# The low halves of the weight tiles: a negated cast and an adding DMA in place of a subtraction

## The chip, the cores and the metric

One core of a Trainium2 chip runs the whole program. Its engines are TensorE (matmul), VectorE, ScalarE and GpSimd; SyncE (SP) only issues transfers here. The metric is the device time of one execution in microseconds.

## The reference

Two layers of a decoder trunk over 512 tokens of width 1024, all in float32. Each layer is a token mixer with three attention branches, three gates and an output projection, and then a channel mixer with a causal convolution of width 3.

```
for i in range(DEPTH):                       # DEPTH = 2
    h = rms_norm(x, attn_norm[i])
    proj = h @ w_in[i]                       # 1024 x 5376
    ...                                      # attention A, B, C: ya, yb, yc
    g = jax.nn.sigmoid(gates.reshape(B, S, N_BRANCH, D))
    merged = g[:, :, 0] * (ya @ w_pa[i]) + g[:, :, 1] * (yb @ w_pb[i]) + g[:, :, 2] * (yc @ w_pc[i])
    x = x + merged @ w_out[i]                # 1024 x 1024
    h = rms_norm(x, mlp_norm[i])
    u = causal_depthwise_conv(h @ w_up[i], conv_w[i], conv_b[i])   # 1024 x 5632
    gate_u, val_u = jnp.split(u, 2, axis=-1)
    x = x + (jax.nn.silu(gate_u) * val_u) @ w_down[i]              # 2816 x 1024
```

Per layer that is 5.4 M weights in w_in, 1 M in the branch projections, 1 M in w_out, 5.8 M in w_up and 2.9 M in w_down, 129 MB in both layers. The rest of the work, the attention, is small at 512 tokens.

## The kernel before, in words

Every float32 operand of a large product is split in two numbers of the type float32r: a high half, the operand rounded to that type, and a low half, operand minus high half. A product is then three matmuls, high by high, high by low and low by high, all added up in PSUM.

Weights come as tiles of 128 x 1024 numbers, 512 KB: for most matrices two groups of 128 rows by 512 columns, for the value columns of w_in four groups by 256, for w_up two groups by two pieces of 256 columns, one from the gate half and one from the value half. There are 246 tiles. `w_dma` has SP load a tile into one of two `raw` buffers, in one transfer, or in two for w_up. `w_prep` makes `whi` by a cast on ScalarE and `wlo` by a subtraction on VectorE or GpSimd; each of the two has four buffers (NW). `dense` walks the blocks of tiles in order and issues, tile by tile, 4 column chunks x 2 row groups x 3 matmuls of 512 columns, so 24 for a tile (48 of 256 columns for the value tiles). At the start of tile i of a block it calls `pump`, which prepares tiles up to i + 2 and has SP load two more.

What runs beside the dense blocks (norms, attention, rotary) are generators. The loop at the end of `trunk` takes the next piece of work from them by an estimate of each engine's clock (class `Estimate`), so the order of instructions on every engine is fixed when the program is built, and a change of an instruction's price in `Estimate.note` moves others. On the chip each engine runs its instructions in that order and waits at each for what it needs.

GpSimd's other work are powers and copies of small statistics: `rn` for the norms (`norm_tail`, line 552), `rr`, `rq`, `nrq`, `rk` for the heads' norms (`rstd_tb`), and the tables of the rotary step. In before all transfers are issued from SP and, for a few constants, ScalarE. The program is opened with room for descriptors of GpSimd's own transfers, in bytes of each partition:

```
nc = _bacc.Bacc("TRN2", target_bir_lowering=False, num_devices=1, dynamic_dma_scratch_size=1024)   # line 1641
```

Nearly every instruction is issued through `Clocked.run`, so the profile puts nearly all of them on line 168 and the names of the tiles tell them apart: `raw`, `whi`, `wlo` are the weights, `d` the PSUM banks of the dense products, `h` the split normed activations, `slot` the general buffers of 128 x 1024, `temp` those of 128 x 512, `tp` and `s` the PSUM of transposes and scores.

Of the kernel before, what the change touches and what calls it, by code (L numbers as in the profile page):

```python
# [11 lines left out]
F32 = mybir.dt.float32  # L12
F32R = mybir.dt.float32r
AF = mybir.ActivationFunctionType
OP = mybir.AluOpType
# [14 lines left out]
POOL_LEAD = 3  # L30
POOL_BIAS = -1000000000.0
# [96 lines left out]
class Bufs:  # L128
# [21 lines left out]
    def any(self, n=1):  # L150
        return len(self.free) >= n
# [3 lines left out]


class Clocked:
    """Runs an engine's instructions and keeps an estimate of when each one ends."""

    def __init__(self, est, eng, key):  # L160
        self._est, self._eng, self._key = est, eng, key
# [12 lines left out]
class Estimate:  # L174
# [60 lines left out]
    def note(self, key, op, args, kw):  # L235
        aps = [x for x in list(args) + list(kw.values()) if isinstance(x, bass.AP)]
        out = kw.get("out", args[0] if args else None)
        if not isinstance(out, bass.AP):
            return
        outs = [out]  # L240
        if "accum_out" in kw and kw["accum_out"] is not None:
            outs.append(kw["accum_out"])
        if op == "tensor_tensor_reduce":
            outs.append(args[-1])
        ins = [x for x in aps if not any(x is o for o in outs)]
        t = self.clock[key]
        for x in ins:
            t = max(t, self.written.get(x.tensor.name, 0.0) + self.SEM)
        for o in outs:
            nm = o.tensor.name  # L250
            if key != "PE" and op != "dma_start":
                t = max(t, self.written.get(nm, 0.0) + (self.SEM if nm in self.written else 0.0))
            if nm[:2] in ("h0", "h1"):
                t = max(t, self.used.get(nm, 0.0) + self.SEM)
            if nm in self.pred:
                t = max(t, self.used.get(self.pred.pop(nm), 0.0) + self.SEM)
        if op == "dma_start":
            self.clock[key] = t + 0.06
            go = max(t + 0.1, self.clock["DGE"])
            self.clock["DGE"] = go + (0.475 if key == "SP" else 0.66)  # L260
            self.clock["DMA"] = max(self.clock["DMA"], go + 1.1) + 1.456 * out.size() / 131072
            end = self.clock["DMA"] + 0.75
        else:
            two = False
            if self.lock and key in ("DVE", "POOL"):
                sb = [x.space != bass.MemoryType.PSUM for x in ins if x.free_size() > 1]
                if key == "POOL":
                    two = any(sb)
                else:
                    two = sum(sb) > 1 or (op in ("tensor_copy", "tensor_scalar") and all(sb)  # L270
                                          and out.space != bass.MemoryType.PSUM)
            if two:
                for s, e in self.port["POOL" if key == "DVE" else "DVE"]:
                    if s <= t < e:
                        t = e
            end = t + self.cost(key, op, out, ins, kw, args)
            self.clock[key] = end
            if two:
                self.port[key].append((t, end))
        self.last = (t, end)  # L280
        for x in ins + outs:
            nm = x.tensor.name
            self.used[nm] = max(self.used.get(nm, 0.0), end)
        for o in outs:
            self.written[o.tensor.name] = max(self.written.get(o.tensor.name, 0.0), end)
# [40 lines left out]
def trunk(ctx: ExitStack, tc: tile.TileContext, out: bass.AP, a: dict):  # L326
    core = tc.nc
    est = Estimate()
# [32 lines left out]
    threads = []  # L361
# [134 lines left out]
    def first_part(t, j):  # L496
        sl = slice(t * 128, (t + 1) * 128)
        ps = tps.get()
        for c in range(4):
            nc.tensor.transpose(ps[:, c, :], X[t][:, (4 * j + c) * 128:(4 * j + c + 1) * 128], identf)  # L500
        for c in range(4):
            k = 4 * j + c
            nc.scalar.activation(H[0, k][:, sl], ps[:, c, :], AF.Copy, scale=gain(0, k))
        for c in range(0, 4, 2):
            nc.scalar.copy(XT[2 * j + c // 2].rearrange("p (e t) -> p e t", e=2)[:, :, sl], ps[:, c:c + 2, :])
        for c in range(4):
            k = 4 * j + c
            nc.vector.scalar_tensor_tensor(H[1, k][:, sl], ps[:, c, :], gain(0, k), H[0, k][:, sl].bitcast(F32),
                                           op0=OP.mult, op1=OP.subtract)
        tps.put(ps)  # L510
# [99 lines left out]
    wt = []  # L610
    W = {}
    RAW = {}
    state = {"dma": 0, "prep": 0, "fin": 0, "busy": False}
# [20 lines left out]
    def w_prep(j):  # L634
        hi = est.alloc("whi", NW, wpool.tile([128, 1024], F32R, tag="whi", name="whi"))
        lo = est.alloc("wlo", NW, wpool.tile([128, 1024], F32R, tag="wlo", name="wlo"))
        raw = RAW.pop(j)
        nc.scalar.copy(hi, raw)
        if state["busy"]:
            t = est.ready(hi)  # L640
            pool = max(est.clock["POOL"], t) <= max(est.clock["DVE"], t) + POOL_BIAS
        else:
            pool = threads[1:] and est.clock["POOL"] <= est.clock["PE"] + POOL_LEAD
        if pool:
            nc.gpsimd.tensor_sub(lo, raw, hi.bitcast(F32))
        else:
            nc.vector.tensor_sub(lo, raw, hi.bitcast(F32))
        if j in wide:
            slots.put(raw)
        if j < 2:  # L650
            first_part(0, j)
        W[j] = (hi, lo)

    def pump(lead):
        while state["prep"] < min(state["fin"] + NW, lead, len(wt)):
            while state["dma"] < min(state["prep"] + ahead(), len(wt)):
                w_dma(state["dma"])
                state["dma"] += 1
            w_prep(state["prep"])
            state["prep"] += 1  # L660
        while state["dma"] < min(state["prep"] + ahead(), len(wt)):
            w_dma(state["dma"])
            state["dma"] += 1
# [888 lines left out]
    def eng_clock(eng):  # L1552
        if eng == "ANY":
            return min(est.clock["ACT"], est.clock["DVE"])
        return est.clock[eng]
# [6 lines left out]
    while threads:  # L1562
# [24 lines left out]
        for r, th in others:  # L1587
            c = eng_clock(th.cur[0])
# [62 lines left out]
```

## Time and profile before

| | us |
|---|---|
| median of the 2 runs | 1603.82 |
| the runs | 1603.31 and 1604.33 |
| span of the profiled execution | 1599.4 |
| busy: TensorE, VectorE, ScalarE, GpSimd | 1546.0, 1077.5, 789.8, 293.6 |

The span goes from the first instruction to the last; the profiled execution's own device time is not listed apart, and the span lies 4.4 us below the median. Busy time of TensorE is that of matmuls that overlap in its pipeline, so 97% busy does not mean 97% of what the engine can do. By stage the program is: layer 0 mixer to about 365 us, gates' end, projections and w_out to about 450, w_up to about 690, w_down to about 810, and the same again for layer 1.

### The profile page before, as it was taken

How to read it: one execution, taken by the hardware profiler on the slowest of the kernel's cores; microseconds unless marked ns; L12 is line 12 of the kernel's file. 1: busy time of each engine (PE TensorE's matmuls, PEld its weight loads, DVE VectorE, ACT ScalarE, POOL GpSimd, SP SyncE). 2: the span in 40 equal slices, each digit the busy share in tenths (PEclk: the TensorE clock that was granted, in tenths of full speed). 3: DMA queues.
4: the chain of work that ended last, by engine and by line, in shares of the span. 5: the costliest groups of instructions: out<-in, count | busy, mean ns of one | idle time of the engine just before them, and what ended most of it. 6: DMA issues, size and time to landing. Idle time of an engine off the chain costs nothing.

```text
span 1599.4 us, 21003 instructions
## 1 busy us (share of the span) xinstructions
PE 1546.0 (97%) x7584; PEld 1283.9 (80%) x7584; DVE 1077.5 (67%) x2242; ACT 789.8 (49%) x1534; POOL 293.6 (18%) x243
## 2 busy tenths in 40 slices
PE   8999999999999999999998999999999999999999
PEld 6777787778878888888887887878788788888887
DVE  5998888988576655543269898797875856665321
ACT  7565656755344444333155666647634544443220
POOL 3443343321010000000044553323200100000000
PEclk9999999999999999999999999999999999999999
DMA  5423152223233233333332224322242233223331
GB/s 176 150 57 90 54 198 67 68 65 132 86 100 100 86 105 106 106 99 125 92 113 66 80 67 158 93 80 64 69 151 87 79 106 93 89 83 106 118 119 53
DMA packets 115495, 157.21 MB, mean 98 GB/s; under 512 B 18880, under 2 KB 71104, under 8 KB 115392
## 3 DMA queue, kind: packets, MB, share of 16 engines
q1 hardware_dynamic: 102768, 153.19, 30.6%
q10 hardware_dynamic: 12624, 2.69, 0.8%
q8 instruction: 60, 0.98, 0.2%
q14 instruction: 43, 0.35, 0.1%
HBM read 144.84 MB, written 11.01 MB: 97 GB/s over the span
## 4 chain that ended last, share of the span: by engine, by line
PE 73%; DVE 20%; ACT 3%; issue 2%; POOL 1%; DMA 0%; ACTq 0%; SPq 0%; DVEq 0%; POOLq 0%
PE d L168 67%; DVE slot L168 8%; PE tp L168 5%; DVE temp L168 4%; DVE s L168 2%; ACT slot L168 2%; DVE nb L168 2%; PE s L168 1%; DVE rl L168 1%; DVE wlo L168 1%; DVE h L168 1%; POOL rr L168 1%; ACT whi L168 1%; ACT temp L168 0%; DMA raw<-in_w_in 0%
## 5 line engine op out<-in xcount | busy, mean ns | idle before, releaser
L168 PE MATMUL d<-h,whi 128*128 128x512 f32 x2176 | 683.0, 395 | 8.6 <-DVE h L168 4.5
L168 PEld LDWEIGHTS d<-h,whi 128*128 128x128 f32 x2176 | 399.9, 189 | 88.5 <-DVE h L168 5.6
L168 PE MATMUL d<-h,wlo 128*128 128x512 f32 x1088 | 425.9, 391 | 0.0
L168 DVE TENSOR_TENSOR wlo<-raw,whi 128x1024 fp32r<-128x1024 f32 x174 | 211.1, 1225 | 263.3 <-ACT whi L168 263.1
L168 ACT CAST whi<-raw 128x1024 fp32r<-128x1024 f32 x246 | 256.1, 1051 | 267.1 <-PE d L168 131.8
L168 PE MATMUL d<-slot,whi 128*128 128x512 f32 x864 | 266.6, 390 | 0.0
L168 POOL TENSOR_TENSOR wlo<-raw,whi 128x1024 fp32r<-128x1024 f32 x72 | 175.5, 2438 | 407.9 <-ACT whi L168 368.0
L168 PEld LDWEIGHTS d<-h,wlo 128*128 128x128 f32 x1088 | 204.9, 188 | 44.0 <-DVE wlo L168 0.2
L168 PE MATMUL d<-whi,h 128*128 128x512 f32 (+1 forms) x768 | 207.4, 344 | 0.4 <-ACT h L168 0.4
L168 PEld LDWEIGHTS d<-slot,whi 128*128 128x128 f32 x864 | 161.6, 188 | 33.3
L168 DVE SCALAR_TENSOR_TENSOR temp<-d,packed,temp 128x511 f32<-128x511 f32 (+1 forms) x176 | 127.8, 747 | 68.3 <-ACT temp L168 65.1
L168 PE MATMUL d<-slot,wlo 128*128 128x512 f32 x432 | 168.2, 389 | 0.0
L168 PEld LDWEIGHTS d<-whi,h 128*128 128x128 f32 x768 | 134.5, 191 | 15.5 <-ACT h L168 0.8
L168 ACT CAST slot<-tp 128x256 fp32r<-128x256 f32 (+3 forms) x289 | 102.4, 377 | 83.5 <-PE tp L168 81.0
L168 PE MATMUL d<-wlo,h 128*128 128x256 f32 (+1 forms) x384 | 130.3, 339 | 0.2 <-DVE wlo L168 0.2
L168 ACT ACTIVATE temp<-d,packed 128x512 f32<-128x512 f32 x88 | 67.8, 772 | 92.8 <-PE d L168 85.1
L168 PE MATMUL d<-whi,slot 128*128 128x512 f32 x352 | 108.4, 389 | 0.0
L168 DVE TENSOR_TENSOR slot<-slot,d 128x512 f32<-128x512 f32 x80 | 54.3, 684 | 71.8 <-PE d L168 68.3
L168 PEld LDWEIGHTS d<-slot,wlo 128*128 128x128 f32 x432 | 81.1, 188 | 16.8
L168 ACT CAST slot<-temp 128x256 fp32r<-128x256 f32 (+2 forms) x140 | 58.1, 455 | 65.8 <-DVE temp L168 65.7
L168 POOL TENSOR_TENSOR rn<-nvs,mhalf 128x4 f32<-128x4 f32 x3 | 3.0, 1007 | 475.8 <-DVE nvs L168 475.8
L168 DVE TENSOR_TENSOR slot<-tp,slot 64x128 fp32r<-64x128 f32 (+4 forms) x180 | 75.8, 425 | 18.7 <-ACT slot L168 16.6
(113 smaller groups left out, 1816.6 us busy)
## 6 DMA issues: line engine op xcount, KB each, us to landing
raw<-in_w_up SPq DMA_DIRECT2D x176, 256.0 KB, 3.2
raw<-in_w_in SPq DMA_DIRECT2D x82, 512.0 KB, 3.7
raw<-in_w_down SPq DMA_DIRECT2D x44, 512.0 KB, 3.7
raw<-in_w_out SPq DMA_DIRECT2D x16, 512.0 KB, 4.4
x_spill<-slot SPq DMA_DIRECT2D x8, 512.0 KB, 4.0
b_parked<-slot SPq DMA_DIRECT2D x8, 512.0 KB, 5.1
slot<-b_parked SPq DMA_DIRECT2D x8, 512.0 KB, 7.1
raw<-in_w_pb SPq DMA_DIRECT2D x8, 512.0 KB, 3.7
```

The source lines that it names most:

```text
L168: r = f(*args, **kw)
```

## The change

`w_prep` no longer subtracts. ScalarE writes `wlo` as the cast of minus the raw tile, which is minus the high half, and GpSimd issues transfers that fetch the float32 weights from memory again and add them to `wlo`: one for each row group (two or four for a tile), and for w_up one for each of the two pieces. The choice between VectorE and GpSimd is gone. In the planner's estimate a transfer from GpSimd costs that engine 1.1 us and does not occupy the hardware queue's issue time.

```diff
         if op == "dma_start":
             self.clock[key] = t + 0.06
+            if key == "POOL":
+                t += 1.1
+                self.clock[key] = t
             go = max(t + 0.1, self.clock["DGE"])
-            self.clock["DGE"] = go + (0.475 if key == "SP" else 0.66)
+            if key != "POOL":
+                self.clock["DGE"] = go + (0.475 if key == "SP" else 0.66)
...
         nc.scalar.copy(hi, raw)
-        if state["busy"]:
-            t = est.ready(hi)
-            pool = max(est.clock["POOL"], t) <= max(est.clock["DVE"], t) + POOL_BIAS
-        else:
-            pool = threads[1:] and est.clock["POOL"] <= est.clock["PE"] + POOL_LEAD
-        if pool:
-            nc.gpsimd.tensor_sub(lo, raw, hi.bitcast(F32))
+        if True:
+            src = wt[j][0]
+            nc.scalar.activation(lo, raw, AF.Copy, scale=-1.0)
+            if len(src) == 1:
+                v = lo.rearrange("p (k c) -> p k c", k=len(wt[j][1]))
+                for k in range(len(wt[j][1])):
+                    nc.gpsimd.dma_start(v[:, k, :], src[0][:, k, :], accum_op=OP.add)
+            else:
+                v = lo.rearrange("p (k g c) -> p k g c", k=2, g=2)
+                for g in range(2):
+                    nc.gpsimd.dma_start(v[:, :, g, :], src[g], accum_op=OP.add)
         else:
             nc.vector.tensor_sub(lo, raw, hi.bitcast(F32))
```

GpSimd's order from the last mixer work of layer 0 to the first of layer 1, before; `wlo` are the tiles that it subtracts, the others of w_out, w_up and w_down being VectorE's:

```order
L168 TENSOR_TENSOR wlo<-raw,whi 128x1024
L168 TENSOR_TENSOR slot_130_2831<-slot_130_2831,vecs 128x4x32 x8
L168 TENSOR_TENSOR wlo<-raw,whi 128x1024 x17
L168 TENSOR_TENSOR rn<-nvs,mhalf 128x4
L168 TENSOR_TENSOR wlo<-raw,whi 128x1024 x2
L168 TENSOR_TENSOR rn<-nvs,mhalf 128x4
L168 TENSOR_TENSOR rr<-vv,mhalf 128x16
L168 TENSOR_SCALAR rqC<-rr 128x8
```

The same place in the changed kernel:

```order
L168 DMA wlo<-in_w_pb 128x512 x8
L168 DMA wlo<-in_w_out 128x512 x16
L168 DMA wlo<-in_w_up 128x2x256 x8
L168 TENSOR_TENSOR rn<-nvs,mhalf 128x4
L168 DMA wlo<-in_w_up 128x2x256 x80
L168 DMA wlo<-in_w_down 128x512 x44
L168 DMA wlo<-in_w_in 128x512 x8
L168 TENSOR_TENSOR rn<-nvs,mhalf 128x4
L168 DMA wlo<-in_w_in 128x256 x8
L168 TENSOR_TENSOR rr<-vv,mhalf 128x16
L168 TENSOR_SCALAR rqC<-rr 128x8
```

All low halves of these stages now go through GpSimd's queue, and the channel norm's `rn` stands behind the first eight pieces of w_up and ahead of the other eighty.

ScalarE in one block of w_up in layer 0, before: the last convolution results of a block (`temp`), the two casts of the block's product (`slot`), the casts of the next four weight tiles:

```order
L168 ACTIVATE temp_85_5641<-d,packed 128x512
L168 ACTIVATE temp_84_5630<-temp_84_5630 128x512
L168 ACTIVATE temp_86_5652<-d,packed 128x512
L168 CAST slot_218_5658<-temp_83_5620 128x512
L168 CAST slot_219_5661<-temp_84_5630 128x512
L168 CAST whi<-raw 128x1024 x4
L168 ACTIVATE temp_87_5774<-d,packed 128x512
```

In the changed kernel, a block of the same stage, up to the first of its four weight tiles:

```order
L168 ACTIVATE temp_106_6634<-d,packed 128x512
L168 CAST slot_228_6640<-temp_103_6602 128x512
L168 CAST slot_229_6643<-temp_104_6612 128x512
L168 CAST whi<-raw 128x1024
L168 ACTIVATE wlo<-raw 128x1024
```

The place among the convolution's instructions is the same; each of the four casts is now followed by a negated one, ahead of the next block's first `temp`.

## Rows read from the trace of the kernel before

**Rows 1.** The page's head and its section 1: busy us, share of span, instructions.

```profile
span 1599.4 us, 21003 instructions
PE 1546.0 (97%) x7584; PEld 1283.9 (80%) x7584; DVE 1077.5 (67%) x2242; ACT 789.8 (49%) x1534; POOL 293.6 (18%) x243
```

**Rows 2.** The chain that ended last: shares of the span by engine, by line.

```profile
PE 73%; DVE 20%; ACT 3%; issue 2%; POOL 1%; DMA 0%; ACTq 0%; SPq 0%; DVEq 0%; POOLq 0%
PE d L168 67%; DVE slot L168 8%; PE tp L168 5%; DVE temp L168 4%; DVE s L168 2%; ACT slot L168 2%; DVE nb L168 2%; PE s L168 1%; DVE rl L168 1%; DVE wlo L168 1%; DVE h L168 1%; POOL rr L168 1%; ACT whi L168 1%; ACT temp L168 0%; DMA raw<-in_w_in 0%
```

**Rows 3.** Windows: mixer of layer 0, w_up; mixer of layer 1, w_up.

```profile
core 0: us, PE busy (x) PEld busy (x) DVE busy (x) ACT busy (x) POOL busy (x), PEclk, DMA share, GB/s
80.00:365.00 285.00, 271.87 (x1511) 226.67 (x1511) 243.07 (x707) 181.09 (x454) 105.23 (x85) 1.00 0.28 86
...
475.00:680.00 205.00, 204.56 (x902) 169.03 (x901) 122.37 (x151) 87.42 (x112) 2.40 (x1) 1.00 0.34 103
811.00:1159.00 348.00, 328.07 (x1822) 276.40 (x1821) 286.76 (x784) 216.21 (x519) 141.94 (x115) 0.99 0.29 86
1266.00:1470.00 204.00, 204.00 (x914) 168.83 (x913) 123.02 (x148) 90.53 (x118) 2.39 (x1) 1.00 0.32 98
```

**Rows 4.** The chain in order of time within w_up of layer 1: start, us, what.

```profile
1299.31 21.81 PE d L168 x96
1321.11 0.44 PE tp L168 x4
1321.55 21.81 PE d L168 x96
```

**Rows 5.** DMA queues (packets, MB, share of 16 engines); issues: KB each, us to landing.

```profile
q1 hardware_dynamic: 102768, 153.19, 30.6%
q10 hardware_dynamic: 12624, 2.69, 0.8%
...
raw<-in_w_up SPq DMA_DIRECT2D x176, 256.0 KB, 3.2
raw<-in_w_in SPq DMA_DIRECT2D x82, 512.0 KB, 3.7
```

**Rows 6.** Groups of instructions by shape: busy us, mean ns; idle before.

```profile
L168 ACT CAST whi<-raw 128x1024 fp32r<-128x1024 f32 x246 | 256.1, 1051 | 267.1 <-PE d L168 131.8 <-DMA raw<-in_w_up 88.3 <-DMA raw<-in_w_down 31.0
L168 DVE TENSOR_TENSOR wlo<-raw,whi 128x1024 fp32r<-128x1024 f32 x174 | 211.1, 1225 | 263.3 <-ACT whi L168 263.1
L168 POOL TENSOR_TENSOR wlo<-raw,whi 128x1024 fp32r<-128x1024 f32 x72 | 175.5, 2438 | 407.9 <-ACT whi L168 368.0 <-PE tp L168 13.7 <-PE d L168 12.2
L168 ACT ACTIVATE slot<-slot 128x1024 f32<-128x1024 f32 x28 | 28.4, 1075 | 0.1
```

**Rows 7.** The chain in order of time at the start of the program.

```profile
8.34 1.13 ACT h L168 x4
12.53 1.89 ACT whi L168 x2
18.65 1.12 DVE h L168 x4
```

**Rows 8.** Instructions of tile raw: SP's issue, ns min/median/max.

```profile
L168 SPq DMA_DIRECT2D raw<-in_w_up x176: 367/411/1396, 420.8 to 1447.9; - x176
```

**Rows 9.** The chain in order of time, head statistics on GpSimd, layer 1.

```profile
824.28 2.91 POOL rr L168
827.84 2.90 POOL rr L168
832.66 3.40 POOL rr L168
```

**Rows 10.** Windows with idle time of TensorE: busy us, granted clock (PEclk).

```profile
40.00:60.00 20.00, 16.87 (x108) 15.32 (x107) 16.77 (x41) 11.41 (x20) 9.97 (x13) 0.91 0.72 221
460.00:470.00 10.00, 7.79 (x32) 5.46 (x31) 9.46 (x15) 6.56 (x10) 0.00 (x0) 1.00 0.03 11
845.00:860.00 15.00, 10.98 (x49) 8.84 (x48) 12.60 (x26) 3.98 (x13) 6.53 (x6) 0.78 0.24 70
```

## The prediction

> **What bounds the kernel now.** I read the page's head first: TensorE is busy for 1546.0 of 1599.4 us, VectorE for 67%, ScalarE for 49%, GpSimd for 18% [rows 1]. The chain of work that ended last is 73% TensorE and 20% VectorE [rows 2]. An average can hide stages, so the windows by stage come next. In the up-projection of either layer TensorE has no idle time worth the name: 204.56 of 205 us, and 204.00 of 204 [rows 3]; VectorE is 60% busy there and ScalarE 43% to 44%. In the mixer stages TensorE idles a little, 13.1 of 285 us in layer 0 and 19.9 of 348 us in layer 1, with VectorE at 85% and 82% [rows 3]. So there are two regimes: a dense one, where only a late weight tile could cost anything, and a mixer one, where VectorE is the second limit.
>
> The pace of the dense regime is in the chain itself: pieces of 96 matmuls of 21.81 us [rows 4], which is one block of four weight tiles, so 5.45 us for a tile. w_up takes 88 of the 246 tiles (176 loads, two for a tile [rows 5], 246 casts [rows 6]), 480 us in all. Whatever delivers less than one w_up tile in 5.45 us takes the place of TensorE as the bound.
>
> **What the change removes.** 174 subtractions of 1.225 us from VectorE and 72 of 2.4 us from GpSimd [rows 6], 211 and 175 us of busy time. In the dense stages this is worth nothing, since these engines were waiting there. In the mixer stages the ceiling is TensorE's idle time, 33 us; what the chain names of it, "DVE wlo" 1% [rows 2], is 16 us. I take 0 for the sum and keep -16 as one end.
>
> **What it adds on ScalarE.** 246 negated casts of 128x1024. The nearest row is an ACTIVATE of that size from SBUF, 1.075 us [rows 6]: 264 us. In the first mixer stage that is at most one for each 5.45 us, 52 of them or 56 us on top of 181 of 285 us, so 83% busy at most, less than VectorE was; in the dense stage 4 x 1.075 per 21.81 us brings ScalarE from 43% to 63%. TensorE's work hides them, with one exception: at the start two casts stand in the chain at 12.53 us [rows 7], each now has a second one behind it, +2 us. Without cover each would cost its 1.075 us, and only where a tile is awaited.
>
> **What it adds on the DMA queues.** Every weight byte is fetched again: SP loads it, and GpSimd then adds it to the negated high half, as two pieces of 256 KB for most tiles (four of 128 KB for the 256-column tiles). The trace before has no DMA issued from GpSimd at all: its two queues of data are SP's and ScalarE's [rows 5]. So the cost has to be bounded.
>
> First as bytes. SP's queue moved 153.19 MB in 30.6% of the engines' time [rows 5], 489 us, so 3.19 us per MB, 1.67 us for a tile of 0.524 MB and 0.84 us for a piece. If an add also reads its destination, it moves each piece's bytes twice, 3.35 us a tile; with the load 5.02 us, just below 5.45. As bytes the change fits, barely.
>
> Then as latency. A 256 KB piece of w_up, loaded by SP, takes 3.2 us from issue to landing [rows 5]. If pieces overlap, that does not matter: tiles are prepared two ahead (line 741), which gives 10.9 us. If they go one after another, a tile takes two of these times and becomes the bound. What decides is how many pieces may be under way. The kernel reserves 1024 bytes per partition for the descriptors of GpSimd's DMAs (line 1641), which is all the room there is for them. A w_up piece is cut into the most runs: two rows of 1 KB in each of 128 partitions, 256 runs, where every other piece has 128. I take it that one w_up piece is under way at a time, and at least two of the others.
>
> [...]
>
> The price of one piece alone: 3.2 us as for SP's load, 0.84 us for the second pass of bytes, and 0.41 us to issue it, SP's own time for one [rows 8]; 4.45, say 4.5 us. Lower end 3.2 us, if reading the destination and issuing cost nothing extra. Upper end 6.1 us: 3.7 us, the landing of a transfer with twice the bytes [rows 5], plus 2.4 us, what GpSimd needs for its longest instruction on a weight tile [rows 6], in place of the issue. I take 4.5 because it is made of rows of the same transfer; the planner's price of 1.1 us for the issue, in the diff, would make it 5.1.
>
> [...]
>
> **The sum.** A w_up tile takes 2 x 4.5 = 9.0 us in place of 5.45; 88 x 3.55 = 312 us. Elsewhere two pieces under way give 2 x 4.5 / 2 = 4.5 us a tile, below 5.45, hidden. GpSimd's other work now stands among the pieces. The channel norm's rn has eight w_up pieces ahead of it, 36 us when they go singly; the block that needs rn awaits the same eight, so I take 0 and at most one piece, 4.5 us, in each layer. The rr steps of 2.90 us, which are in the chain after 824 us [rows 9], could each wait for a piece that is queued ahead; most stand in a row of their own with no piece between, so 0, at most +10. The span of 1599.4 us stands 4.4 below the median of 1603.8; I add to the median: 1603.8 + 312 + 2 = 1918, say **1920 us**.
>
> **Rivals.**
> First, pieces overlap in w_up as well (or the issue path is quick enough). It decides at 2.7 us per piece: below that a tile is there within 5.45 us and TensorE is the bound again. Then only the small terms are left, from 1603.8 - 16 + 2 = 1590 to 1630 us, not slower. For it: SP's loads plainly overlap, two pieces per tile at a pace of 5.45 us with landings of 3.2. Against it: the 1024 bytes.
>
> Second, the adding itself is slow, and all 246 tiles pay. With an add moving at k times a load's time, a tile needs 1.67 x (1 + k) us of the sixteen engines and binds beyond k = 2.25. At k = 4 it is 8.4 us, 246 x 8.4 = 2066, with starts and other traffic about 2120 us. For it: nothing in the trace adds. [...]
>
> Third, TensorE's clock. Where it waits, its granted clock has been lower: 0.78 in a stretch with 10.98 of 15 us busy and 0.91 with 16.87 of 20, though 1.00 with 7.79 of 10 [rows 10]. After the change it would be busy 5.45 of 9.0 us. [...]
>
> **How the numbers follow.** One piece at a time: 0.66, from 1604 + 88 x (6.4 - 5.45) = 1688 to 1604 + 88 x (12.2 - 5.45) = 2198 us. Overlap: 0.12. Slow adding: 0.13. Clock: 0.09. A difference of 2% is 32 us, about what a measurement of this kernel can tell from no change. The first rival is nearly all within it, with 0.02 for a gain beyond; the other three cases are slower. Faster 0.02, same 0.09, slower 0.89. The range 1690 to 2190 us leaves out the first rival and the far half of the slow adding, about 0.2 with the tails.
>
> **What would show it.** GpSimd's queue would stand in the table of DMA queues with some 129 MB. In the w_up stages TensorE would be about 60% busy, a group of 96 matmuls would come every 36 us, its idle time would be laid to wlo's DMA, and pieces would start about 4.5 us apart, each after the one before has landed. In w_down, with 44 tiles, TensorE should stay full at 5.45 us a tile; if it idles there as much, the second rival is right. [...] VectorE should lose 211 us, and the mixer stages stay within 16 us of what they were. I am wrong if w_up pieces start less than 2.7 us apart, or if w_down and the gates slow down too.

## The result

The changed kernel takes 2128.27 us (median of 2 runs, 2125.87 and 2130.67) where before took 1603.82: a ratio of 1.3273, 95% interval 1.3248 to 1.3298. The forecast was 1920 us with a range of 1690 to 2190. Its sign held, and its mechanism for w_up; it was 208 us too low.

The page of the changed kernel: head, busy time, the chain's shares, the two large queues, and of its tables of groups and issues the rows of the new work (issues: KB each, median us to landing).

```profile
span 2123.9 us, 21924 instructions
PE 1713.8 (81%) x7584; PEld 1358.6 (64%) x7584; DVE 790.1 (37%) x2116; ACT 1007.4 (47%) x1733; POOL 627.5 (30%) x691
...
q0 software_dynamic: 97408, 130.06, 39.2%
q1 hardware_dynamic: 102768, 153.19, 23.9%
...
PE 37%; issue 26%; DMA 11%; ACT 9%; POOL 9%; DVE 7%; ACTq 0%; SPq 0%; POOLq 0%; DVEq 0%
...
L168 POOL DMA_DIRECT2D wlo<-in_w_up x176 | 214.3, 1218 | 734.1 <-issue 539.4
L168 ACT ACTIVATE wlo<-raw 128x1024 fp32r<-128x1024 f32 x246 | 259.9, 1056 | 0.0
...
raw<-in_w_up SPq DMA_DIRECT2D x176, 256.0 KB, 3.4
wlo<-in_w_up POOLq DMA_DIRECT2D x176, 256.0 KB, 4.5
...
wlo<-in_w_down POOLq DMA_DIRECT2D x88, 256.0 KB, 6.2
```

TensorE's share of the chain fell from 73% [rows 2] to 37%, and what took its place is "issue", 26%: time in which an engine stood at an instruction and the profile shows nothing that it waited for. GpSimd's row says whose: 539.4 us of idle time ahead of the 176 w_up transfers end in "issue". The new queue carries 130.06 MB, which is 248 tiles of 0.524 MB; the 246 of the sections above is the count of casts out of `raw`, and two more tiles come through `slot`.

The waits of the changed kernel (engine, tile, what it waited for: us in total, times, longest):

```profile
POOL wlo L168 <- issue: 688.7, 224, 6.7
...
PE d L168 <- DMA wlo<-in_w_up: 256.9, 141, 6.3
...
PEld d L168 <- DMA wlo<-in_w_up: 239.5, 112, 5.2
```

TensorE waits for `wlo` of w_up, 256.9 us at the matmul and much of it again at the weight load. GpSimd's timeline in w_up of layer 0 shows why (start us, us, what, idle before and what ended it):

```profile
643.22 1.21 POOL L168 DMA_DIRECT2D wlo<-in_w_up  x1 [4.23 <-issue]
647.89 1.21 POOL L168 DMA_DIRECT2D wlo<-in_w_up  x1 [3.46 <-issue]
652.92 1.21 POOL L168 DMA_DIRECT2D wlo<-in_w_up  x1 [3.82 <-ACT temp L168]
657.66 1.20 POOL L168 DMA_DIRECT2D wlo<-in_w_up  x1 [3.52 <-issue]
662.35 1.23 POOL L168 DMA_DIRECT2D wlo<-in_w_up  x1 [3.49 <-ACT wlo L168]
669.06 1.21 POOL L168 DMA_DIRECT2D wlo<-in_w_up  x1 [5.49 <-issue]
```

The fastest follow each other at 4.67 us, which is the landing of 4.5 and a little. Of the 176 pieces none starts before the one ahead of it has landed: one piece is under way at a time. The windows of w_up (layer 0, layer 1) and of w_down say what that does to the stage (columns as in [rows 3]):

```profile
500.00:700.00 200.00, 129.62 (x470) 95.37 (x470) 53.00 (x79) 67.24 (x84) 47.09 (x40) 0.86 0.52 97
...
1500.00:1700.00 200.00, 137.60 (x497) 103.63 (x496) 52.94 (x80) 69.03 (x87) 43.57 (x37) 0.83 0.52 101
...
955.00:1065.00 110.00, 107.87 (x474) 88.40 (x473) 7.12 (x11) 45.24 (x49) 37.02 (x43) 1.00 0.95 214
```

In w_up TensorE was busy for all of 205 us [rows 3] and now is for 65 to 69%, while the DMA engines are half idle (0.52): the limit there is a latency, not bytes. In w_down, where the pieces have half as many runs, TensorE is busy for 107.87 of 110 us and the DMA engines are nearly full (0.95).

Dividing the span by stage settles where the 524.5 us of added span lie. The times run from the first dense matmul (one that writes `d`) of a stage to the first of the next; a mixer holds w_in and the branch projections and everything beside them.

| us | mixer 0 | w_out 0 | w_up 0 | w_down 0 | mixer 1 | w_out 1 | w_up 1 | w_down 1 |
|---|---|---|---|---|---|---|---|---|
| before | 385.2 | 43.5 | 245.1 | 119.7 | 381.0 | 43.5 | 249.0 | 119.5 |
| after | 417.9 | 55.0 | 464.6 | 123.7 | 404.8 | 54.5 | 460.6 | 128.9 |

w_up has 431 us of it, the mixers 56.5, w_out 22.5, w_down 13.4. The experiments go through these in turn.

### The profile page after: what moved, and what is told of

Its sections match the earlier page's. It is cut to its first block, busy times and chain, and to the rows that moved or that the text cites. A ratio compares the mean times of both kernels' runs of the same rounds, so it can differ in the third digit from the quotient of the medians.

```text
span 2123.9 us, 21924 instructions
## 1 busy us (share of the span) xinstructions
PE 1713.8 (81%) x7584; PEld 1358.6 (64%) x7584; DVE 790.1 (37%) x2116; ACT 1007.4 (47%) x1733; POOL 627.5 (30%) x691
## 3 DMA queue, kind: packets, MB, share of 16 engines
q0 software_dynamic: 97408, 130.06, 39.2%
## 4 chain that ended last, share of the span: by engine, by line
PE 37%; issue 26%; DMA 11%; ACT 9%; POOL 9%; DVE 7%; ACTq 0%; SPq 0%; POOLq 0%; DVEq 0%
PE d L168 31%; POOL wlo L168 6%; PE tp L168 4%; DMA wlo<-in_w_up 4%; DVE temp L168 4%; ACT whi L168 3%; ACT wlo L168 2%; DVE slot L168 2%; DMA wlo<-in_w_in 2%; ACT slot L168 2%; POOL rr L168 2%; DMA wlo<-in_w_down 2%; PE s L168 1%; DMA wlo<-in_w_out 1%; DMA raw<-in_w_up 1%
## 5 line engine op out<-in xcount | busy, mean ns | idle before, releaser
L168 PE MATMUL d<-h,whi 128*128 128x512 f32 x2176 | 754.2, 430 | 5.5 <-ACT h L168 3.5
L168 PE MATMUL d<-h,wlo 128*128 128x512 f32 x1088 | 482.2, 443 | 280.0 <-DMA wlo<-in_w_up 256.9
L168 PEld LDWEIGHTS d<-h,whi 128*128 128x128 f32 x2176 | 447.2, 210 | 98.6 <-ACT h L168 4.2
L168 PEld LDWEIGHTS d<-h,wlo 128*128 128x128 f32 x1088 | 226.4, 208 | 397.5 <-DMA wlo<-in_w_up 239.5
L168 POOL DMA_DIRECT2D wlo<-in_w_up x176 | 214.3, 1218 | 734.1 <-issue 539.4
L168 POOL DMA_DIRECT2D wlo<-in_w_in x192 | 171.4, 1040 | 376.1 <-ACT slot L168 123.1
L168 ACT ACTIVATE wlo<-raw 128x1024 fp32r<-128x1024 f32 x246 | 259.9, 1056 | 0.0
L168 ACT CAST slot<-tp 128x256 fp32r<-128x256 f32 (+3 forms) x267 | 95.6, 376 | 77.0 <-PE tp L168 70.1
L168 POOL DMA_DIRECT2D wlo<-in_w_down x88 | 77.6, 908 | 146.9 <-ACT wlo L168 76.5
L168 PEld LDWEIGHTS d<-wlo,h 128*128 128x128 f32 x384 | 74.9, 195 | 31.2 <-DMA wlo<-in_w_in 17.0
```

What stands on the lines that cost most here:

```text
L168: r = f(*args, **kw)
```

## Experiments on w_up

**Room for two pieces.** The descriptor room is 1088 bytes in place of 1024. So that the 64 bytes fit, a scratch tile is dropped and a short set-up instruction writes over its operand.

```diff
-nc = _bacc.Bacc("TRN2", ..., dynamic_dma_scratch_size=1024)
+nc = _bacc.Bacc("TRN2", ..., dynamic_dma_scratch_size=1088)
```

> The changed kernel with 1088 bytes of room for descriptors of GpSimd's transfers in place of 1024 (paid for by a scratch tile of 128 bytes whose products now overwrite their first operand). Theory: a w_up piece waits for the one before because only one fits the room; two fit now, so pieces overlap, start at most 2.7 us apart, and the two w_up stages fall from 465 and 461 us to 245 to 290 each, the whole to 1700 to 1790 us. Rival, the adding itself is slow: pieces under way share the same rate, period stays 5.2 us, 2110 to 2140 us. Rival, the order of GpSimd's queue (it waits for ScalarE before each pair of pieces): no change, 2110 to 2140 us.

Measured: 1795.02 us, ratio to before 1.1214 (1.1195 to 1.1233). Sixty-four bytes give back 333 us; w_up takes 297.0 and 292.1 us, every other stage within about 3 us of what it took in the changed kernel. GpSimd's timeline in the same stage:

```profile
616.22 1.21 POOL L168 DMA_DIRECT2D wlo<-in_w_up  x1 [5.02 <-issue]
618.33 1.22 POOL L168 DMA_DIRECT2D wlo<-in_w_up  x1 [0.90 <-issue]
621.00 1.21 POOL L168 DMA_DIRECT2D wlo<-in_w_up  x1 [1.46 <-ACT wlo L168]
622.98 1.22 POOL L168 DMA_DIRECT2D wlo<-in_w_up  x1 [0.76 <-issue]
```

Pieces start 2.0 to 2.7 us after one another although each now takes 5.2 us to land, and 160 of the 176 start before the one ahead has landed. That one piece was under way at a time, for want of room, is shown.

**Smaller pieces, the old room.** Each w_up piece is issued as two of 128 KB, by row group, so that more than one may go into 1024 bytes.

```diff
-                    nc.gpsimd.dma_start(v[:, :, g, :], src[g], accum_op=OP.add)
+                    for k in range(2):
+                        nc.gpsimd.dma_start(v[:, k, g, :], src[g][:, k, :], accum_op=OP.add)
```

> The changed kernel with each w_up tile added in four pieces of 128 KB (128 runs each) in place of two of 256 KB (256 runs), room unchanged. Theory (room counted in runs): at least two, likely three pieces under way; a 128 KB piece landed 4.5 us after issue in the value columns, so a tile takes 4 x 4.5 / 3 = 6.0 us to 4 x 4.5 / 2 = 9.0 us in place of 10.4, the whole 1740 to 2010 us. Rival, slow adding by bytes: the same bytes, 2110 to 2140 us. Rival, pieces always go singly whatever their size: 4 x 4.5 = 18 us a tile, 2790 us or more.

Measured: 1792.19 us (1 run); w_up 292.8 and 293.9 us. Its pieces of w_up land in 4.0 us (median) and overlap: the five from 640.4 to 646.8 us start 1.2 to 2.7 us after one another. The same result with the room untouched, so it is not the room as such but whether the next piece fits beside the one under way.

**Copying in place of adding, pieces one at a time.** Room of 512 bytes, in which the pieces went alone, and w_up's pieces copied over the negated half: the sum of w_up's low halves is left out.

```diff
-                    nc.gpsimd.dma_start(v[:, :, g, :], src[g], accum_op=OP.add)
+                    nc.gpsimd.dma_start(v[:, :, g, :], src[g])
...
-nc = _bacc.Bacc("TRN2", ..., dynamic_dma_scratch_size=1024)
+nc = _bacc.Bacc("TRN2", ..., dynamic_dma_scratch_size=512)
```

> The room cut to 512 bytes, and w_up's second transfers copy the weights over the negated halves in place of adding (the low halves of w_up are then the weights themselves; the sum is left out); all other tiles add as in the change. It measures one piece alone, plain and adding. Theory: any piece of this size now goes singly. A plain w_up piece saves the second pass of bytes, 0.84 us: period 4.4, w_up 385 us a layer; adding pieces of 128 runs cost what w_up's cost, 5.2 us, so w_down, hidden before, takes 22 x 10.4 = 229 us; the whole 2450 to 2600 us. If an add costs no more than a copy, w_up stays at 460 us. If it is the number of runs that made w_up's pieces slow, w_down takes 120 to 160 us and the whole stays below 2200 us.

Measured: 2484.63 us (1 run); w_up 360.9 and 360.3 us, and now w_down 216.7 and 223.8. Its issues of w_up and w_down:

```profile
wlo<-in_w_up POOLq DMA_DIRECT2D x176, 256.0 KB, 3.3
...
wlo<-in_w_down POOLq DMA_DIRECT2D x88, 256.0 KB, 4.1
```

In its timeline w_up's pieces start 3.5 us or more after one another (700 to 740 us), w_down's 4.0 or more (1060 to 1117 us). Alone, a plain piece lands in 3.3 us and an adding one, in the changed kernel, in 4.5: the adding costs 1.2 us. From start to start it is 4.1 us against 5.2 (means over all pieces of a layer). w_down, little harmed at 1024 bytes, nearly doubles when its pieces too must go singly: 216.7 / 44 = 4.9 us a piece. So in the changed kernel w_down is spared because at least two of its 128-run pieces fit; there 82 of its 88 start before the one ahead has landed, and up to three are under way.

**Is it bytes, once pieces overlap?** At 1088 bytes w_up is still 52 and 43 us above before. Four times the room (one `slot` buffer given up), and then that with a third `raw` buffer (two given up), so that neither descriptors nor loads are short:

```diff
-NSLOT = 33
-RAW_BUFS = 2
+NSLOT = 31
+RAW_BUFS = 3
...
-nc = _bacc.Bacc("TRN2", ..., dynamic_dma_scratch_size=1024)
+nc = _bacc.Bacc("TRN2", ..., dynamic_dma_scratch_size=4096)
```

The one with more room alone:

> The changed kernel with 4096 bytes of room for GpSimd's descriptors and 32 general buffers in place of 33 to pay for it. Theory: with seven pieces in the room the landing no longer sets the pace, w_up returns to 245 to 260 us in each layer, the whole to 1690 to 1720 us, give or take 10 for the lost buffer. Rival, the transfers' bytes bind once pieces overlap (two in the room gave 297 and 292 us): w_up stays at 285 to 300 us, the whole 1775 to 1800 us.

The one with the third buffer too:

> As the run with 4096 bytes of room, with three raw buffers in place of two and 31 general buffers in place of 32. With room for seven pieces w_up still took 288 us a layer, not 245. Theory, a loop of latencies: SP may load only when a raw buffer is read twice by ScalarE, the load takes 6.1 us and the adding 8.7 us there; a third buffer starts loads a tile earlier, w_up 245 to 268 us. Rival, the DMA engines' rate binds (83% busy there): 282 to 292 us. The whole 1700 to 1770 us, with the lost buffers' cost in the mixers unknown.

Measured: 1770.06 and 1747.66 us (1 run each), w_up 287.9 and 288.0, then 288.2 and 283.7. A piece then takes 8.7 and 11.0 us to land, and the stage hardly moves: more under way only takes longer to land. The theory of each run, that the room or the loads still limited w_up, falls. Last, the kernel with 1088 bytes with w_up's pieces copied, not added; the sum of w_up's low halves is left out.

> The kernel with 1088 bytes of descriptor room, with w_up's pieces copied over the negated half instead of added to it; the sum of w_up's low halves is left out, all else is the same. With 1088 bytes w_up took 297 and 292 us and the transfers kept the DMA engines busy 0.82 of the time. Theory (it is the adding, the second pass over the destination, that fills the DMA engines there): copied, a tile's load and second fetch are two plain transfers of 0.84 us a piece, 3.4 us a tile, TensorE sets the pace again: w_up of 245 to 255 us a layer, DMA share of at most 0.6, in all 1700 to 1720. Rival (GpSimd's transfers are slow whatever they do, by their issue, their descriptors or their short room): w_up stays at 275 to 297, in all 1760 to 1800.

Measured: 1714.82 us (1 run), w_up 254.6 and 255.0. The windows of w_up in layer 0, first with the adding:

```profile
490.00:770.00 280.00, 247.82 (x1032) 199.10 (x1031) 96.20 (x141) 143.78 (x176) 104.58 (x87) 0.96 0.82 161
```

and copied:

```profile
490.00:720.00 230.00, 223.33 (x975) 182.03 (x976) 92.30 (x136) 136.64 (x169) 59.89 (x83) 0.99 0.72 191
```

A w_up tile takes 297.0 / 44 = 6.75 us with the adding, of which the sixteen DMA engines are busy 0.82, 5.5 us. Copied it is 5.79 us at 0.72, 4.2 us. It is the adding that holds w_up there, and what it takes is time of the DMA engines. The copied pieces may also take less of the room, but more room alone left w_up at 288 us. The copy is not free either, 255 us against 245, and its share of 0.72 is above the 0.6 that was expected.

## Experiments on the other stages

**w_up left as before.** w_up's low halves are subtracted, the other tiles' added by DMA.

```diff
+        if len(wt[j][0]) == 1:
             nc.scalar.activation(lo, raw, AF.Copy, scale=-1.0)
...
+        elif pool:
+            nc.gpsimd.tensor_sub(lo, raw, hi.bitcast(F32))
         else:
             nc.vector.tensor_sub(lo, raw, hi.bitcast(F32))
```

> The changed kernel with w_up's low halves subtracted as before, all other tiles by negated cast and adding transfer. Theory: the w_up stages lose what they gained, 431 us, and only the rest of the loss stays, 90 us, most of it in the mixers: 1690 to 1705 us. If instead the other stages lost time only because w_up's queue of pieces reached into them, it is 1610 to 1640 us. If the adding is slow everywhere, w_down (124 and 129 us) and the gates get slower once w_up no longer holds the loads back: above 1720 us.

Measured: 1699.33 us, ratio 1.0612 (1.0596 to 1.0627). w_up is back at 245.1 and 248.9, and what stays is 99 us in the other stages, against 92 in the changed kernel: mixers 422.8 and 405.2, w_out 55.1 and 54.7, w_down 124.0 and 129.9. The two losses are nearly independent.

**No adding DMA at all.** The negated cast stays, and VectorE or GpSimd adds the raw tile to it, as they subtracted before.

```diff
+        nc.scalar.activation(lo, raw, AF.Copy, scale=-1.0)
+        if pool:
+            nc.gpsimd.tensor_add(lo, raw, lo.bitcast(F32))
+        else:
+            nc.vector.tensor_add(lo, raw, lo.bitcast(F32))
```

> No adding transfers at all: ScalarE's negated cast stays, and VectorE or GpSimd, chosen as before, adds the raw tile to it in place of subtracting. It isolates ScalarE's 264 us. Theory: they are hidden by TensorE's work, 1604 to 1620 us. Rival: they are what made the mixer stages 33 and 24 us slower, 1650 to 1665 us.

Measured: 1669.02 us, ratio 1.0418 (1.0402 to 1.0433). The theory, that ScalarE's extra casts cost nothing, fell: with no transfer added, the mixers take 413.2 and 405.5 us and w_up 252.8 and 255.5. But this edit changes two things, since the planner is told of the casts and plans everything anew: the order on every engine, and in part which engine does what. The next two runs part them. In one the work is that of the kernel just told and the planner is told the old costs, which leaves the order of before; in the other the planner counts a cast that is never issued, which gives the new order with the work of before.

```diff
+        core.scalar.activation(lo, raw, AF.Copy, scale=-1.0)
...
+        (core.gpsimd if pool else core.vector).tensor_add(lo, raw, lo.bitcast(F32))
+        est.note("POOL" if pool else "DVE", "tensor_sub", (lo, raw, hi.bitcast(F32)), {})
```

> As the run with a negated cast and an added raw tile, but the planner is told nothing of the second cast: the order of every engine's instructions is that of the kernel before, with a negated cast behind each cast on ScalarE. It separates ScalarE's time from the order that the planner makes of it. Theory A, ScalarE's own time in the mixers costs the 67 us: 1640 to 1670 us. Theory B, the planner's other order costs them: 1600 to 1620 us.

```diff
+        est.note("ACT", "activation", (lo, raw, AF.Copy), {"scale": -1.0})
+        (core.gpsimd if pool else core.vector).tensor_sub(lo, raw, hi.bitcast(F32))
+        est.note("POOL" if pool else "DVE", "tensor_add", (lo, raw, lo.bitcast(F32)), {})
```

> The other half of the pair: the planner counts a second cast on ScalarE that is never issued, and the subtraction is that of the kernel before. The order is that of the run with the negated cast and the added raw tile, the work that of the kernel before. Theory A: 1600 to 1620 us. Theory B: 1650 to 1670 us.

Measured: work without the order 1632.76 us, ratio 1.0198 (1.0181 to 1.0216), mixers 395.7 and 391.8; order without the work 1658.96 us, ratio 1.0359 (1.0339 to 1.0379), mixers 409.8 and 404.5. The first lies between the ranges of its two theories, the second meets theory B. The planner's other order alone, with not one instruction added, costs 24 us a mixer. It contains a choice of engine too: 24 small copies and scalings of ScalarE and five subtractions of GpSimd go to VectorE. The work costs some 10 us a mixer when an engine must still wait behind both casts. The two do not add up: apart they cost 57 and 31 us, together 68, so part of one hides behind the other.

**The adding DMA in the order of before.** w_up subtracted, the other tiles added by DMA, the planner told the costs of before.

```diff
+            core.scalar.activation(lo, raw, AF.Copy, scale=-1.0)
...
+                    core.gpsimd.dma_start(v[:, k, :], src[0][:, k, :], accum_op=OP.add)
...
+            est.note("POOL" if pool else "DVE", "tensor_sub", (lo, raw, hi.bitcast(F32)), {})
```

> w_up subtracted as before, all other tiles by negated cast and adding transfers, and the planner told the costs of the kernel before, so that every engine keeps that kernel's order around the changed instructions. Beside the run with w_up subtracted (1699 us) it takes away the planner's new order alone. Theory, from the pair of runs on ScalarE (24 us a layer by order, 10 by work): the mixers fall by 15 to 30 us each, the whole to 1640 to 1670 us. Rival, the adding transfers' own latency and GpSimd's queue make the mixers slow: 1685 to 1705 us.

Measured: 1669.32 us, ratio 1.0421 (1.0403 to 1.0438). Against the kernel with w_up subtracted the order gives back 12 us in the first mixer (410.5) and 27 in the second (378.5), which ends at or below before's 381.0. These are stages of the profiled execution, which at 1661.85 us is the fastest of the five; by the medians it is 30 us for both mixers together. w_out (53.9, 54.2) and w_down (124.1, 130.2) do not move, so their loss is the transfers' own. What is left in the first mixer is its start; its first 100 us, and below them its waits there:

```profile
0.00:100.00 100.00, 68.23 (x329) 55.17 (x329) 36.71 (x118) 58.74 (x121) 43.62 (x59) 0.85 0.74 183
```

```profile
PE d L168 <- DMA wlo<-in_w_in: 22.5, 6, 7.3
POOL wlo L654 <- issue: 21.8, 10, 4.8
```

**The adding DMA only where it should be free.** As the last, but only for the tiles of w_in from the nineteenth tile of the program on.

```diff
-        if len(wt[j][0]) == 1:
+        if j >= 18 and wt[j][0][0].tensor.name == "in_w_in":
```

> The adding transfer only for the gate tiles of w_in from the nineteenth tile of the program on; every other low half is subtracted as before, and the planner goes by the costs of before, so that the order is that of before. Theory (away from the program's start, from w_out, w_up and w_down the change costs nothing, and VectorE's relief is worth a few us a layer): 1593 to 1606 us, mixers of 377 to 386 and 372 to 381 us between their first matmul and that of w_out. Rival (ScalarE's second cast or late landings cost in the mixers themselves, some 10 us a layer as in the kernel with the negated cast and the order of before): 1610 to 1630, mixers of about 392 to 396.

Measured: 1601.22 us (11 runs) against 1602.36 (15 runs), ratio 1.0000 (0.9991 to 1.0009); mixers 386.9 and 377.6. Its page, and its first 100 us, now subtracted again:

```profile
PE 1543.5 (97%) x7584; PEld 1284.7 (80%) x7584; DVE 987.3 (62%) x2225; ACT 848.6 (53%) x1600; POOL 297.5 (19%) x342
...
wlo<-in_w_in POOLq DMA_DIRECT2D x116, 256.0 KB, 5.8
...
wlo<-in_w_in POOLq DMA_DIRECT2D x32, 128.0 KB, 4.3
```

```profile
0.00:100.00 100.00, 85.90 (x453) 70.73 (x454) 75.68 (x200) 63.98 (x158) 33.65 (x37) 1.00 0.45 141
```

Sixty-six tiles go the new way and VectorE has 90 us less to do [rows 1]; the longer way of these tiles and the relief come together to no cost and no gain, and they were not tried apart. In the first 100 us TensorE has 85.9 us of matmuls in place of 68.2: the start costs 17.7 us, and the first mixer as a whole 410.5 - 386.9 = 23.6, in which the branch projections' tiles are as well. No kernel here beats before.

## Why the prediction was right, and where its sum was off

**One w_up piece at a time: right.** This step carried the forecast. The room of 64 bytes more, and pieces of half the size in the old room, each give back over 330 us, and the timelines show single starts in the one case and overlapping ones in the other. What a piece takes of the room no run counts. That one w_up piece goes at a time, and at least two of the others, was the author's estimate from the 256 and 128 runs; the runs show one w_up piece under way with 1024 bytes and more than one with 1088, up to three pieces of 128 runs with 1024, and one with 512. If the room is shared out by size, a w_up piece takes more than 512 bytes of it and at most 544, an estimate from the runs with 1024 and 1088 bytes. That the time fell within the range is in part luck: the range was made of the price of a piece alone, and the 92 us that other stages lost were in none of its bounds.

**The price of a piece: the term that was mis-sized.** 4.5 us a piece gave 9.0 a tile and +312 us. Measured it is 5.2 us from start to start, 464.6 / 44 = 10.6 us a tile, and +431. The landing of a lone piece did come out at 4.5 us, but by two errors that cancel: a plain piece lands in 3.3 us, as SP's in 3.2 [rows 5]; the adding costs 1.2 us, not 0.84, of which 0.5 is its longer issue (1.22 us against 0.72), and whether it reads its destination, as the 0.84 took it, no run shows; and the 0.41 us for the issue was not to be added, since the issue lies inside the landing.

What failed is the step from this landing to the pace: that every piece lands as if it were alone and that the next starts at that moment. The landings in w_up have a median of 4.5 us but a mean of 4.86, and the next piece starts 0.36 us after a landing (mean; the median is 0.32, the smallest too). That makes the 5.2. The 73 pieces with no load of SP's beside them land in 4.5 us, the 18 with six such loads beside them in 6.4. One of the slow ones, in the chain of the changed kernel, and what SP issues at that time:

```profile
661.44 0.91 issue
662.35 1.23 POOL wlo L168
663.58 5.47 issue
```

```profile
661.45 8.02 SPq L168 DMA_DIRECT2D raw<-in_w_up  x6
```

The piece of 662.35 holds the next one up for 5.47 us in place of 3.4 to 3.5. ScalarE's negated cast, behind which a pair of pieces stands, hardly matters: all waiting beyond the 0.32 us adds up to 4 us in a layer. That the loads beside a piece are what makes it slow is read from the trace and was not tried apart.

**"As bytes the change fits, barely": wrong.** 5.02 us a tile was estimated, below 5.45. Measured it is 5.5 us of DMA time, and over w_up of layer 0 the share of the engines is 0.82 with 1088 bytes, 0.83 with 4096 and 0.84 with the third `raw` buffer (the last two from 520 to 720 us). So with the rooms tried w_up ends at some 284 to 297 us: the first rival, pieces that overlap, would not have led to 1590 to 1630 us but leaves w_up alone, with all room and a third buffer, 43.1 + 34.7 = 78 us above before. This did not touch the forecast, but the rival's time was off. Why the share stops there, when in w_down it reaches 0.95, stays open; the pieces of w_up are cut in runs of 1 KB, those of w_down of 2 KB.

**"Elsewhere hidden", 0: wrong by 92 us.** This is the second term that failed, in four parts. The signs that the prediction named, mixers within 16 us of before and no slowing of w_down and the gates, did not hold: the mixers lost 33 and 24 us, w_down 4 and 9.
- The start: +2 us was taken for two casts. The late thing is not ScalarE but the transfer: the first tiles are awaited with nothing to cover them, and TensorE waits 22.5 us for `wlo` in the kernel with the order of before (14.2 in the changed kernel). The whole of it is about 18 to 24 us.
- The order: the text showed that a price in the planner moves other instructions, and gave that no term. It is 24 us a mixer when tried alone, with the plan that one more cast for each tile gives; read from the order given back with the transfers in place, 12 and 27 us, or 30 for both by the medians. For layer 1 that is about all of the mixer's loss of 24.
- w_out: 11 us in each layer, where TensorE had no idle time before. The chain between 400 and 485 us in the changed kernel has both transfers in it:

```profile
434.58 9.53 DMA raw<-in_w_out
446.25 7.30 DMA raw<-in_w_out
458.84 8.52 DMA wlo<-in_w_out
```

  A load of SP's that lands in 6.2 us (median of 16) feeds a cast, and the cast a piece of 6.4; a tile awaits both in a row. That this series is the cause is argued from the chain alone, and one run speaks against the load's part: with a third `raw` buffer, which lets SP load earlier, w_out still takes 53.9 and 53.7 us.
- w_down: +4 and +9 us. Inside the stage TensorE stays full, as forecast; the loss is at its beginning and at the turns of its blocks, where the chain has single waits of 7.2 and 7.7 us for `wlo`.

**ScalarE's casts, 0: right in the order of before.** There the second mixer is 378.5 us with all its casts. They cost 10 us a mixer, and some 4 in each w_up, where VectorE's add must still wait behind both. In the planner they did cost: their price is what gave the other order.

**VectorE's relief, 0: right as far as shown.** 16 us was the end of the range; 90 us less work in the mixers, with 66 casts and their adding transfers in its place and the order kept, is 0.0% (0.9991 to 1.0009). A relief of a few us that the new work takes back is not excluded. Over the changed kernel VectorE lost 287 us of work and not 211, for which see the last section.

**GpSimd's other work.** For rn at most 4.5 us a layer was taken. TensorE's waits for it are longer, up to 19.2 us and 41.3 in three, but in w_up they run while the eight pieces ahead go through one by one, which the block awaits too; no run tells them apart.

**The other rivals.** Slow adding everywhere is refuted: w_down takes 123.7 / 22 = 5.6 us a tile at 0.95 of the DMA engines, not 8.4. The clock: it was granted at 0.83 to 0.88 in w_up and TensorE still stood idle for 60 to 70 of 200 us, so it did not set the pace.

## What to carry to other kernels

A transfer that takes over an engine's work had two prices here, its bytes and its turn. One w_up piece under way at a time, 88 of them at 5.2 us from start to start, made a stage of 465 and 461 us with the DMA engines busy for 0.52 to 0.55 of it; with several under way it was 284 to 297 us at 0.82 to 0.84. So find out from the timeline how many transfers the reserved room lets start before the first has landed; if it is one, take its latency, as it is beside the other loads, times their number as the estimate of the stage's time. Work taken from an engine that is not the last one awaited bought little here: 0.0% for 90 us, net of the work that took its place. Look at who is late in each stage first, and at the starts, where nothing covers a longer chain: at that of this program it cost 17.7 us. And where a planner orders the program, run the new costs alone and the new work alone before either is blamed.

## What was not expected of the hardware

- An adding piece of 256 KB costs 1.2 us more than a plain one when alone (landing 4.5 against 3.3 us), of which 0.5 is its longer issue, and with pieces overlapping it raises the DMA engines' time of a w_up tile from 4.2 to 5.5 us.
- The issue of a transfer did not occupy GpSimd for the same time in each: 1.22 us for an adding w_up piece, 0.87 (median) for an adding w_down piece with half as many runs, 0.72 for a plain w_up piece. With 4096 bytes of room adding w_up pieces issued in a row took about the same each: two in 2.47 us, four in 4.91.
- Some of VectorE's instructions with both operands in SBUF took far longer before, and no longer do in the changed kernel. Of one shape before:

```profile
L168 DVE TENSOR_TENSOR slot<-slot,slot 128x512 f32<-128x512 f32 x53 | 45.0, 849 | 1.1
```

  and after:

```profile
L168 DVE TENSOR_TENSOR slot<-slot,slot 128x512 f32<-128x512 f32 x53 | 36.6, 690 | 1.1
```

  849 ns became 690, and an instruction of 128x128 with two such operands went from 398 to 296 ns, while those that read PSUM stayed as they were (684 and 685 ns). The trace of before shows where the 849 come from. Of the 53, the 46 that run beside no GpSimd instruction take 689 ns on average. Seven run beside one of GpSimd's subtractions of 2.4 us [rows 6] and take 1903; six of these seven had found it running, and each ended 0.55 us after it.
